# Another line for the time of a TensorE product in a kernel that orders its own instructions

## The chip, the cores and the metric

The kernel runs on one core of a Trainium2 chip. The number that counts is the device time of one execution in microseconds (us), as the median of several runs.

## What is computed

The kernel makes one inference step of a trunk of four layers, for 512 prompt frames and 32 sample frames side by side. Each layer normalises and modulates its input, mixes tokens, adds the result to the residual, normalises again and applies a gated feed forward (FFN). Layers 0 and 3 mix by differential attention, layer 1 by an mLSTM, layer 2 by latent attention.

```python
def trunk(x, c, past, p):
    ...
    for i in range(DEPTH):
        kind, j = i % N_MIXERS, i // N_MIXERS
        mod = (jax.nn.silu(c) @ p['w_ada'][i] + p['b_ada'][i])[:, None, :]
        sh1, sc1, gt1, sh2, sc2, gt2 = jnp.split(mod, 6, axis=-1)
        h = rmsnorm(x, p['g_norm1'][i]) * (1.0 + sc1) + sh1
        ...
        x = x + gt1 * out
        h = rmsnorm(x, p['g_norm2'][i]) * (1.0 + sc2) + sh2
        x = x + gt2 * swiglu(h, p['w_ffn_in'][i], p['w_ffn_out'][i])
    y = rmsnorm(x, p['g_final'])
```

## The kernel before

**Tiles.** Activations lie with features on the 128 partitions and the 544 frames along the row. A row is worked in two halves (`HALVES`): half 0 has 256 frames, half 1 has 288. Every operand of a large product is kept as a high and a low part (`hh` and `hl` for the input of a projection, `wh` and `low` for a weight), and `prod` issues three TensorE products for one K tile: high by high, low by high, high by low. A projection of one output tile and one half is 8 K tiles, so 24 products, added up in one PSUM bank (`mm`, `S` or `O` in the names).

**Norms.** `Norm.add` squares each new residual tile (`sq`) and sums it (`ss`). When the last output tile of a half is in the residual, `final_norm_task` is spawned with the highest priority. Its first step, `Norm.rstd`, makes two products with a matrix of constants (`T<-ss,ones_d` and `T<-sq,ones_d`), which add over the partitions; ScalarE makes `rs` of that, and `Norm.column` makes `ht`, `hh` and `hl`, one K tile at a time, on VectorE and ScalarE. In a mixer's output projection the last tiles go half by half, so the norm of half 0 is made while half 1 is still being projected, and the norm of half 1 while the FFN's first products on half 0 run. Those first products are a pair of PSUM tiles, 48 products on half 0.

**Who sets the order.** All of it is written by a scheduler in the kernel's own code. `Sched.run` holds the tasks, which are generators that issue TensorE's work, and an estimated time `t`. At each step it takes, among the tasks whose operands are estimated to be ready at `t`, the one of highest priority, and lets it issue its next products. `Tensor._held` estimates how long one product holds TensorE and moves `t` on by that. The instructions of VectorE (DVE), ScalarE (ACT) and GpSimd (POOL) get the first free time after their operands by `Engine.cost`, DMAs by their size. At the end of a phase everything noted is issued in the order of its estimated time. On the chip each engine then works through its own list in that order and waits on semaphores: an instruction that is not ready holds up those behind it on its engine, and the estimate plays no further part.

The norm's two products are asked for with `t_need`, which is a free bank and the time at which `ss` and `sq` are estimated to be written:

```python
    def final_norm_task(norm, i, finish):
        a, b = HALVES[i]
        yield t_need(norm.ss[:, a:b], norm.last[a][:, : b - a])
        yield from finish(norm, i)
```

**Other places named below.** In the mLSTM layer, `gates` is a long chain of small operations on VectorE and ScalarE; `turn_gates` and `sample_setup` bring its results through TensorE (`b_decb`, `hTl`, `b_rowsS`, `b_ash`). At the start, `warm_up` issues products without a use while the first loads come in, until the estimated time passes 16 us.

Of the kernel before, what the change touches and what calls it, by code (L numbers as in the profile page):

```python
# [13 lines left out]
PSUM = bass.MemoryType.PSUM  # L14

P = 128
# [35 lines left out]
def EARLY(h, z):  # L52
    """How many of the first conditioning's tiles are made after a projection."""
    return 0 if h == 0 else 2 if z == 2 and h < 4 else 1


class Sched:
    """An order of all engines' work, from an estimate of when each instruction can run.

    Tasks are generators that issue the tensor engine's work; each yields when its next step can start: None or a  # L60
    function that gives the time. The other engines' instructions take the first free time after their operands.
    Instructions are noted first and issued by their time, a phase at once.
    """
# [29 lines left out]
    def later(self, gen):  # L93
        """Work that only takes time that is left: yields its engine, what it reads and its cost, then notes it."""
        self.idle.append([gen, next(gen)])
# [17 lines left out]
    def flush(self):  # L113
        """Issues what is noted, in the order of its time."""
        self.log.sort(key=lambda a: a[:2])
        for _, _, issue in self.log:
            issue()
        self.log = []
        for eng, rows in self.busy.items():
            self.floor[eng] = max([self.floor.get(eng, 0.0)] + [b for _, b in rows])  # L120
# [7 lines left out]
    # what is known of a tile: (first and last partition, first and last column, time)  # L128
# [42 lines left out]
    def free(self, key, bufs):  # L171
        """When a new tile of a ring can be written."""
# [3 lines left out]
    def ready(self, *aps):  # L176
        """When the tensor engine can read."""
# [9 lines left out]
    def hole(self, eng, t, cost, take=True):  # L187
        """The first free time of an engine, from t on."""
# [60 lines left out]
class Engine:  # L249
    """An engine whose instructions are noted with their time."""  # L250
# [50 lines left out]
class Tensor:  # L301
    """The tensor engine, with an estimate of how long it is held."""
# [4 lines left out]
    def _held(self, out, lhs, rhs, passes, issue, turn=False):  # L307
# [8 lines left out]
        else:  # L316
            cost = max(passes * m / 2400.0, m / 1200.0, passes * n / 2400.0) + 0.0025
# [18 lines left out]
def tile_trunk(ctx: ExitStack, tc: tile.TileContext, I, O):  # L336
# [31 lines left out]
    class Banks:  # L368
        """PSUM banks for products and turned tiles, each use in the one that is free first.

        A bank for turned tiles is written and read before another one is asked for; one for products is shut.
        """
# [47 lines left out]
    def t_need(*aps):  # L420
        """A bank for turned tiles, and the operands."""
# [8 lines left out]
    def s_pool(es, shape, bufs):  # L430
        """Two PSUM banks of one phase: a pair in one tile, or one after the other."""
# [43 lines left out]
    # ---------------------------------------------------------------- loads  # L475
# [46 lines left out]
    # ---------------------------------------------------------------- weights  # L522
    def all_weights():
        """Every loaded weight, in the order of its use; some are split by GpSimd, where VectorE has much else to do."""
# [44 lines left out]
    class Feed:  # L569
        """Weights, loaded and split in place as soon as those before them are used up; some stay as they are."""  # L570
# [4 lines left out]
        def first(self, n):  # L575
            """The first ones' tiles; who takes them loads and splits them."""
# [55 lines left out]
    def units(us, started=False):  # L632
        """us: [(psum, parts)] side by side, one K tile of each at a time."""
# [21 lines left out]
    # ---------------------------------------------------------------- adaLN rows  # L655
# [5 lines left out]
    def ada_rows(ps, raw, first=0):  # L661
        """Four sums over K tiles in rows 32 g + (prompt, sample)."""
# [46 lines left out]
    # ---------------------------------------------------------------- residual and norms  # L709
    class Norm:  # L710
# [26 lines left out]
        def half(self, i, am, sh, silu=False):  # L737
            """The normed, modulated input of the next products: high and low parts of one half."""
# [33 lines left out]
    class Cycle:  # L772
        """PSUM banks in turn where no attention needs its own."""
# [18 lines left out]
    def out_block(load, drop, parts, gt, get, order, norm=None, finish=None, gate=None):  # L792
        """One block of K tiles of an output projection, added to the residual."""
# [26 lines left out]
    def paired():  # L820
        """K blocks of four tiles, two output tiles to a load: how to get one and how to drop it."""
# [15 lines left out]
    # ---------------------------------------------------------------- feed forward  # L837
# [80 lines left out]
    # ---------------------------------------------------------------- attention helpers  # L918
    def row_softmax(pool, ps, n, nk, scale, outs, masked):
        """ps: [P, n, >=nk] scores; outs[s] = exp(scale * (S - row max)); returns 1 / row sums."""  # L920
# [15 lines left out]
    def times_v(pool, pr, v, po):  # L936
        """po[dv, q] = sum over keys of v[key, dv] * pr[qt][q, key], 128 keys at a time."""
# [21 lines left out]
    def sample_times_v(p, vs, lock, pt, out):  # L959
        """p: [(h, q), 288] -> PSUM [(h, q), dv]; vs: [P, 3, 4, P] (last block: the new 32 keys)."""  # L960
# [18 lines left out]
    class Progress:  # L979
        """What has been issued, for the tasks that wait for it."""  # L980
# [21 lines left out]
    def rope_task(pool, pr, key, ps, i, hi, lo, r, perm, cos, sin, bufs=2):  # L1002
        """ps: one half of a projection; its rotation goes through the tensor engine in two exact parts."""
# [29 lines left out]
    # ---------------------------------------------------------------- differential attention  # L1033
    def layer_a(l, j, finish, early, first):
        lam_init = 0.8 - 0.6 * math.exp(-0.3 * l)
        with ExitStack() as es:
# [32 lines left out]
            def first_rows(k):  # L1069
                """The weights that make scale and shift of one K tile."""  # L1070
# [6 lines left out]
            def first_column(k, parts, am, norm):  # L1077
                """Scale and shift of one K tile, from the conditioning; then that tile of the input."""
# [1327 lines left out]
```

## Time and profile before

| | us |
|---|---|
| median of 3 runs (2749.83 to 2750.35) | 2750.12 |
| span of the profiled execution | 2748.0 |
| TensorE busy in it | 2705.6 |
| VectorE busy in it | 1820.7 |
| ScalarE busy in it | 1086.5 |

The span runs from the first to the last instruction of the core and is 2.1 us under the median of the runs, which also count what lies around it. TensorE's products overlap: a product of 256 columns shows about 0.28 us from start to end while its neighbour starts long before it ends. So its rate is read from the distance of two starts, and its waits from the idle time in front of an instruction, not from the busy share.

### The profile page before, as it was taken

What the parts mean: (1) busy time and instruction counts of PE and PEld (TensorE: products, weight loads), DVE (VectorE), ACT (ScalarE), POOL (GpSimd) and SP (SyncE); (2) the same over time, 40 slices, a digit from 0 to 9 for tenths busy, and PEclk for the clock granted to TensorE, in tenths of its full rate; (3) what the DMA queues carried; (4) which work ended last, traced back from release to release, by engine and by line L of the source; (5) the groups of instructions that cost most, each with busy time, mean ns of one, the idle gap of its engine ahead of it and who ended that gap; (6) DMA issues with size and microseconds to landing.
All of it is one profiled execution on the core that took longest, in us unless ns stands there. A gap on an engine that the chain in (4) does not pass through costs nothing.

```text
span 2748.0 us, 51869 instructions
## 1 busy us (share of the span) xinstructions
PE 2705.6 (98%) x21223; PEld 2590.8 (94%) x21223; DVE 1820.7 (66%) x3621; ACT 1086.5 (40%) x2382; POOL 238.0 (9%) x242
## 2 busy tenths in 40 slices
PE   9999999999999999999999999999999999999998
PEld 6888899999999999999998899999998899999998
DVE  6878777777665677777366767777558887433333
ACT  4555442122466442223255534222235554321222
POOL 1000300000200120000110020000031112000001
PEclk9999999999999999999999999999999999999999
DMA  8343244555222235455221124555333222222221
GB/s 281 129 139 123 87 153 164 187 172 180 87 83 78 76 110 174 170 183 176 80 97 33 47 78 142 170 181 177 126 108 97 77 80 75 77 88 90 88 86 68
DMA packets 101461, 330.94 MB, mean 120 GB/s; under 512 B 12840, under 2 KB 20140, under 8 KB 100840
## 3 DMA queue, kind: packets, MB, share of 16 engines
q1 hardware_dynamic: 95976, 309.48, 33.6%
q0 software_dynamic: 5248, 18.14, 1.8%
q8 instruction: 167, 2.74, 0.4%
q14 instruction: 70, 0.57, 0.1%
HBM read 314.69 MB, written 12.89 MB: 119 GB/s over the span
## 4 chain that ended last, share of the span: by engine, by line
PE 90%; DVE 6%; ACT 2%; issue 1%; DMA 0%; DVEq 0%; SPq 0%; ACTq 0%
PE mm L329 54%; PE S L329 21%; PE O L329 11%; PE T L329 2%; PE T L332 2%; DVE ht L296 1%; DVE hl L296 1%; DVE x L296 1%; ACT hh L296 1%; ACT wh L296 0%; DVE low L296 0%; DVE rq L296 0%; DVE mx L296 0%; DVE ql L296 0%; ACT rs L296 0%
## 5 line engine op out<-in xcount | busy, mean ns | idle before, releaser
L329 PE MATMUL mm<-hh,wh 128*128 128x288 f32 (+1 forms) x3078 | 909.8, 296 | 0.5 <-ACT hh L296 0.4
L329 PE MATMUL mm<-hh,low 128*128 128x288 f32 (+1 forms) x3078 | 887.9, 288 | 0.0
L329 PE MATMUL mm<-hl,wh 128*128 128x288 f32 (+1 forms) x3078 | 884.5, 287 | 2.2 <-DVE hl L296 2.2
L329 PEld LDWEIGHTS mm<-hh,wh 128*128 128x128 f32 x3078 | 580.7, 189 | 22.3 <-issue 15.1
L329 PEld LDWEIGHTS mm<-hl,wh 128*128 128x128 f32 x3078 | 581.8, 189 | 2.6 <-DVE hl L296 2.6
L329 PEld LDWEIGHTS mm<-hh,low 128*128 128x128 f32 x3078 | 581.1, 189 | 3.3 <-issue 2.4
L296 ACT CAST wh<-raw 128x1024 fp32r<-128x1024 f32 (+2 forms) x392 | 399.9, 1020 | 335.7 <-PE mm L329 159.4
L296 DVE TENSOR_TENSOR low<-raw,wh 128x1024 fp32r<-128x1024 f32 (+2 forms) x358 | 421.8, 1190 | 153.4 <-ACT wh L296 152.0
L329 PE MATMUL S<-hh,wh 128*128 128x288 f32 (+1 forms) x892 | 257.5, 289 | 0.5 <-ACT hh L296 0.5
L329 PE MATMUL S<-hl,wh 128*128 128x288 f32 (+1 forms) x892 | 256.6, 288 | 1.0 <-DVE rq L296 1.0
L329 PE MATMUL S<-hh,low 128*128 128x288 f32 (+1 forms) x892 | 257.3, 288 | 0.0
L329 PE MATMUL mm<-uh,wh 128*128 128x288 f32 (+1 forms) x836 | 241.3, 289 | 0.0
L329 PE MATMUL mm<-uh,low 128*128 128x288 f32 (+1 forms) x836 | 240.5, 288 | 0.0
L329 PE MATMUL mm<-ul,wh 128*128 128x288 f32 (+1 forms) x836 | 239.9, 287 | 0.0
L296 ACT CAST uh<-uf 128x256 fp32r<-128x256 f32 (+1 forms) x176 | 73.9, 420 | 406.1 <-DVE uf L296 405.9
L296 DVE SCALAR_TENSOR_TENSOR x<-mm,mod,x 128x256 f32<-128x256 f32 (+1 forms) x278 | 103.7, 399 | 163.3 <-PE mm L329 162.4
L296 POOL TENSOR_TENSOR ss<-ss,sq 128x256 f32<-128x256 f32 (+1 forms) x80 | 75.6, 945 | 1537.2 <-ACT sq L296 1536.9
L296 DVE CUSTOM_DVE_ANT_0 ada<-ada,sc,bada 128x1024 f32<-128x1024 f32 x152 | 194.7, 1281 | 2.6
L296 DVE CUSTOM_DVE_ANT_0 junk<-ada,sc,bada 128x1024 f32<-128x1024 f32 x152 | 194.5, 1280 | 1.0 <-DMA ada<-in_w_adaT 0.9
L329 PEld LDWEIGHTS S<-hh,wh 128*128 128x128 f32 x892 | 167.5, 188 | 2.8 <-issue 2.1
L329 PEld LDWEIGHTS S<-hl,wh 128*128 128x128 f32 x892 | 168.1, 189 | 1.8 <-DVE rq L296 1.3
L329 PEld LDWEIGHTS S<-hh,low 128*128 128x128 f32 x892 | 167.6, 188 | 0.0
(487 smaller groups left out, 5212.5 us busy)
## 6 DMA issues: line engine op xcount, KB each, us to landing
raw<-in_w_fin SPq DMA_DIRECT2D x176, 512.0 KB, 3.3
ada<-in_w_adaT SPq DMA_DIRECT2D x152, 512.0 KB, 4.5
raw<-in_w_fo SPq DMA_DIRECT2D x64, 512.0 KB, 3.3
raw<-in_w_qkv SPq DMA_DIRECT2D x45, 512.0 KB, 3.8
raw<-in_w_ada SPq DMA_DIRECT2D x24, 512.0 KB, 3.7
raw<-in_w_fl SPq DMA_DIRECT2D x32, 384.0 KB, 3.1
raw<-in_w_bh SPq DMA_DIRECT2D x24, 512.0 KB, 3.5
raw<-in_w_ao SPq DMA_DIRECT2D x16, 512.0 KB, 3.6
```

The source lines that it names most:

```text
L296: return s.work(self.kind, outs, ins, self.cost(name, args, kw, outs, ins), lambda: f(*args, **kw))
L329: lambda: self.pe.matmul(out, lhsT, rhs, start=start, stop=stop))
L332: self._held(out, in_, ident, 0, lambda: self.pe.transpose(out, in_, ident), True)
```

## The change

One line of `Tensor._held` is replaced. It is the estimate for every product of the split operands and for the wide products in full precision; the lines for turning a tile and for the narrow conditioning products stay. For 256 columns the estimate goes from 0.109 to 0.118 us, for 288 columns from 0.1225 to 0.132 us. All other differences of the two files are comments and docstrings.

```diff
         elif m <= 32 and passes == 4:
             cost = 0.02 + 0.053 * n / P
         else:
-            cost = max(passes * m / 2400.0, m / 1200.0, passes * n / 2400.0) + 0.0025
+            cost = max(passes * m / 2400.0, m / 1200.0, passes * n / 2265.0) + 0.005
         s = self.sched
         if s.t < COLD:
             cost *= 2
```

The instructions are the same, but for 8 of the `warm_up` products at the start, which are no longer issued (20754 products in place of 20762). What moves is the order, in nearly all of the mixers' stretches on every engine. Three places follow, with rows of each engine's list (source line, operation, output<-inputs with the tile's number, size of the output).

**From a mixer to its FFN, TensorE (first layer).** `mm_1044` is the last tile of the output projection, half 1; `mm_4770` and `mm_4771` (then `mm_4762` and `mm_4763`) are the FFN's first pair on half 0. Before:

```order
L329 MATMUL mm_4771<-hh,wh_1025 128x256
L329 MATMUL mm_4771<-hh,low_66 128x256
L329 MATMUL mm_4771<-hl,wh_1025 128x256
L329 MATMUL T_4772<-ss_1001,ones_d 128x288
L329 MATMUL T_4772<-sq_1046,ones_d 128x288
L329 MATMUL mm_4770<-hh,wh_1000 128x256
L329 MATMUL mm_4770<-hh,low_65 128x256
L329 MATMUL mm_4770<-hl,wh_1000 128x256
L329 MATMUL mm_4771<-hh,wh_1025 128x256
L329 MATMUL mm_4771<-hh,low_66 128x256
L329 MATMUL mm_4771<-hl,wh_1025 128x256
L329 MATMUL mm_4778<-hh,wh_1032 128x256
```

In the changed kernel:

```order
L329 MATMUL mm_4763<-hh,wh_1025 128x256
L329 MATMUL mm_4763<-hh,low_66 128x256
L329 MATMUL mm_4763<-hl,wh_1025 128x256
L329 MATMUL T_4764<-ss_1001,ones_d 128x288
L329 MATMUL T_4764<-sq_1046,ones_d 128x288
L329 MATMUL mm_4762<-hh,wh_1000 128x256
L329 MATMUL mm_4762<-hh,low_65 128x256
L329 MATMUL mm_4762<-hl,wh_1000 128x256
L329 MATMUL mm_4763<-hh,wh_1025 128x256
L329 MATMUL mm_4763<-hh,low_66 128x256
L329 MATMUL mm_4763<-hl,wh_1025 128x256
L329 MATMUL mm_4762<-hh,wh_1000 128x256
```

The norm's two products stood behind 42 of the pair's 48 products and stand now behind 30 of them: 12 products earlier, with 18 of the pair left behind them in place of 6. The same counts hold in all four layers.

**The same place, VectorE.** These are the last instructions ahead of and including the sum `ss` that the norm's product reads. Before:

```order
L296 TENSOR_TENSOR low_68<-raw_62,wh_1039 128x1024
L296 SCALAR_TENSOR_TENSOR ht_1042<-x,amod_1019,rs_1002 128x256
L296 SCALAR_TENSOR_TENSOR x<-mm_1041,mod_97,x 128x256
L296 SCALAR_TENSOR_TENSOR x<-mm_1044,mod_97,x 128x32
L296 SCALAR_TENSOR_TENSOR hl<-ht_1042,mod_97,hh 128x256
L296 SCALAR_TENSOR_TENSOR x<-mm_1044,mod_97,x 128x256
L296 TENSOR_TENSOR ss_1001<-ss_1001,sq_1043 128x288
```

In the changed kernel:

```order
L296 TENSOR_TENSOR low_68<-raw_62,wh_1039 128x1024
L296 SCALAR_TENSOR_TENSOR ht_1041<-x,amod_1019,rs_1002 128x256
L296 SCALAR_TENSOR_TENSOR x<-mm_1042,mod_97,x 128x256
L296 SCALAR_TENSOR_TENSOR x<-mm_1042,mod_97,x 128x32
L296 SCALAR_TENSOR_TENSOR hl<-ht_1041,mod_97,hh 128x256
L296 SCALAR_TENSOR_TENSOR x<-mm_1044,mod_97,x 128x256
L296 TENSOR_TENSOR ss_1001<-ss_1001,sq_1043 128x288
```

One small residual step changes its place. From the first `ht` of half 0 to this sum VectorE has 32 instructions before and 32 of the same kinds now, in each of the four layers.

**From an FFN to the next mixer, TensorE (into the mLSTM).** `mm_9072` to `mm_9074` are the mixer's first three tiles on half 0. Before:

```order
L329 MATMUL mm_9074<-hl,wh_5151 128x256
L329 MATMUL mm_9072<-hh,wh_5138 128x256
L329 MATMUL mm_9072<-hh,low_67 128x256
L329 MATMUL mm_9072<-hl,wh_5138 128x256
L329 MATMUL T_9076<-ss_5108,ones_d 128x288
L329 MATMUL T_9076<-sq_5160,ones_d 128x288
```

In the changed kernel, where the tiles are `mm_9068` to `mm_9070`:

```order
L329 MATMUL mm_9070<-hh,wh_5144 128x256
L329 MATMUL mm_9070<-hh,low_63 128x256
L329 MATMUL mm_9070<-hl,wh_5144 128x256
L329 MATMUL T_9071<-ss_5100,ones_d 128x288
L329 MATMUL T_9071<-sq_5153,ones_d 128x288
L329 MATMUL mm_9068<-hh,wh_5130 128x256
```

The pair stands 3 products earlier: 27 products lie between the FFN's last product and it, where there were 30. The same holds at all three such places.

## Rows read from the trace of the kernel before

**Rows 1.** The page: span, and busy time by engine (share of span).

```profile
span 2748.0 us, 51869 instructions
PE 2705.6 (98%) x21223; PEld 2590.8 (94%) x21223; DVE 1820.7 (66%) x3621; ACT 1086.5 (40%) x2382; POOL 238.0 (9%) x242
```

**Rows 2.** Busy time by stretch: start, mixer 0, FFN 0, mixer 3.

```profile
core 0: us, PE busy (x) PEld busy (x) DVE busy (x) ACT busy (x) POOL busy (x), PEclk, DMA share, GB/s
0.00:50.00 50.00, 48.00 (x339) 33.45 (x339) 26.87 (x96) 24.63 (x65) 9.26 (x17) 1.00 0.92 315
50.00:342.00 292.00, 285.25 (x2440) 253.50 (x2440) 241.03 (x589) 154.60 (x419) 35.60 (x39) 1.00 0.36 125
342.00:740.00 398.00, 397.15 (x3165) 396.87 (x3166) 285.99 (x461) 120.32 (x195) 18.02 (x17) 1.00 0.48 161
2048.00:2339.00 291.00, 280.84 (x2132) 254.53 (x2130) 246.22 (x555) 156.62 (x407) 59.53 (x57) 1.00 0.26 85
```

**Rows 3.** TensorE's waits by releaser: first four and last of 20.

```profile
engine line waited for: us in total, times, longest us
PE T L329 <- DVE ss L296: 12.9, 4, 3.3
PE T L329 <- DVE xl L296: 4.2, 7, 1.2
PE mm L329 <- DVE hl L296: 2.2, 2, 2.0
PE T L329 <- ACT sq L296: 1.8, 4, 0.7
...
PE T L329 <- ACT on L296: 0.3, 1, 0.3
```

**Rows 4.** TensorE in time order, mixer to FFN, layers 0 to 3.

```profile
start us, us, engine line op out<-in xcount [idle before <-releaser]
339.39 0.28 PE L329 MATMUL mm<-hl,wh 128*128 128x256 f32 x1
342.85 0.72 PE L329 MATMUL T<-ss,ones_d 128*128 128x288 f32 x2 [3.18 <-DVE ss L296]
343.68 0.49 PE L329 MATMUL mm<-hh,wh 128*128 128x256 f32 x1
...
996.50 1.03 PE L329 MATMUL T<-ss,ones_d 128*128 128x288 f32 x2 [3.32 <-DVE ss L296]
...
1650.51 0.72 PE L329 MATMUL T<-ss,ones_d 128*128 128x288 f32 x2 [3.24 <-DVE ss L296]
...
2339.49 1.30 PE L329 MATMUL T<-ss,ones_d 128*128 128x288 f32 x2 [3.19 <-DVE ss L296]
```

**Rows 5.** Busy time from the first `ht` to the `ss` sum, layers 0 to 3.

```profile
324.70:342.70 18.00, 14.96 (x118) 14.76 (x116) 17.88 (x32) 9.78 (x19) 10.72 (x9) 1.00 0.51 176
978.40:996.40 18.00, 14.78 (x117) 14.57 (x115) 17.84 (x33) 9.83 (x19) 11.06 (x9) 1.00 0.51 176
1632.40:1650.40 18.00, 14.86 (x118) 14.66 (x116) 17.84 (x32) 9.82 (x19) 11.04 (x9) 1.00 0.50 176
2321.30:2339.30 18.00, 15.01 (x118) 14.80 (x116) 17.84 (x32) 9.75 (x20) 10.70 (x8) 0.97 0.36 118
```

**Rows 6.** TensorE in time order inside FFN 0: starts of products, back to back.

```profile
384.83 0.30 PE L329 MATMUL mm<-hh,low 128*128 128x288 f32 x1
...
385.77 0.30 PE L329 MATMUL mm<-hl,wh 128*128 128x288 f32 x1
...
390.76 0.28 PE L329 MATMUL mm<-hh,low 128*128 128x256 f32 x1
...
391.94 0.28 PE L329 MATMUL mm<-hl,wh 128*128 128x256 f32 x1
```

**Rows 7.** TensorE at the first FFN's end, into the mLSTM.

```profile
740.94 0.75 PE L329 MATMUL T<-sq,ones_d 128*128 128x288 f32 x2 [0.33 <-ACT sq L296]
```

**Rows 8.** TensorE behind the mLSTM's gates.

```profile
776.71 0.25 PE L329 MATMUL T<-b_ash,b_selHr 4*128 4x32 f32 x1 [0.51 <-DVE b_tm L296]
```

**Rows 9.** Busy time and granted clock behind the waits of rows 4 and 8.

```profile
342.90:346.40 3.50, 3.50 (x26) 3.29 (x27) 2.37 (x4) 2.40 (x5) 1.11 (x3) 1.00 0.79 267
996.80:1000.20 3.40, 3.40 (x13) 2.91 (x12) 1.48 (x3) 1.62 (x3) 0.54 (x1) 0.50 0.84 296
1650.60:1654.00 3.40, 3.40 (x25) 3.19 (x26) 2.27 (x3) 2.31 (x4) 1.04 (x2) 1.00 0.72 258
2338.20:2345.00 6.80, 5.50 (x21) 4.96 (x22) 4.57 (x8) 4.56 (x9) 2.49 (x3) 0.50 0.00 0
778.30:785.10 6.80, 6.80 (x33) 6.80 (x33) 3.99 (x7) 3.25 (x6) 0.00 (x0) 0.50 0.12 26
```

## Prediction

> **What bounds the kernel now.** The page comes first: TensorE is busy for 98% of the span, VectorE for 66%, ScalarE for 40% [rows 1]. So VectorE and ScalarE matter only where TensorE waits for them, and the table by stretch says where that can be. In the first FFN TensorE is busy for 397.15 of 398.00 us; an order can win or lose nothing there. In the first mixer it is 285.25 of 292.00 and in the last 280.84 of 291.00 [rows 2]. Third, the list of who TensorE waited for: 20 kinds of wait that sum to 31.5 us. One kind alone is 12.9 us, four waits of up to 3.3 us for the sum `ss` on VectorE, and the next is 4.2 us in 7 waits [rows 3]. Fourth, these four waits in time order: they stand where a mixer hands over to its FFN, once in each layer [rows 4]. All that a new order can work on is 31.5 us of waits, the time at half clock that follows some of them, and new waits.
>
> **What the four waits are.** In rows 4 TensorE starts a product on half 0 of the FFN at 339.39 and then the norm's product at 342.85. The products behind it run at once afterwards; their input was there, but TensorE's list is worked in order. So the wait is not for want of work. It is there because the norm's product stands too early in the list. Its operand is late because VectorE has 32 instructions from the first `ht` to the sum, and they take exactly 18.00 us in each of the four layers, with VectorE busy for 17.84 to 17.88 of them [rows 5]. The moment at which `ss` is written is therefore set by VectorE's own list, not by TensorE.
>
> **The estimate against the trace.** In the FFN, ten products of 256 columns lie between the starts 390.76 and 391.94, so 0.118 us each; seven of 288 between 384.83 and 385.77, so 0.134 us [rows 6]. The old line says 0.109 and 0.1225, the new one 0.118 and 0.132: the new line is right about TensorE. But a scheduler that puts a waiting product in the list when its operand should be ready counts that delay in products. A slower TensorE means fewer products in the same delay, so everything that waits for another engine moves forward by some 8%, while the other engines' costs stay as they were. Where these are already too short, as at the four waits, the old error made up for part of it.
>
> [...]
>
> **The sum, part by part.**
>
> 1. Mixer to FFN, four times. The norm's products move forward by 12 products. VectorE has the same 32 instructions in both orders, so `ss` is not earlier, and TensorE gets there 12 x 0.118 = 1.42 us sooner and waits that much longer: about 4.7 us in place of 3.3. The 12 products are still to be done behind the wait, so nothing comes back, unless TensorE waited again at the end of half 0; it has no such wait now (the FFN stretch is busy but for 0.85 us, most of it this wait's end). 4 x 1.42 = **+5.7 us**. Bounds: 0 if VectorE's chain became shorter by as much, 6 if it became longer a little.
>
> 2. FFN to mixer, three times. The norm's products move forward by 3. The `sq` product waits 0.33 us there now [rows 7], so it is already at the edge: 3 x 3 x 0.118 = **+1.1 us**, between 0 and 1.1.
>
> 3. The mLSTM's gates. Of the 24 products of the tile ahead of `b_decb`, 18 stood in front of it and now 9 do, so TensorE comes up to 9 x 0.134 = 1.2 us earlier. The long gate chain is already waited for (0.51 us at 776.71) [rows 8]. Between 0 and 1.2; I take **+0.6 us**.
>
> 4. The clock. [...] The idle times were 3.32 and 3.19 us with the fall, 3.18 and 3.24 us without [rows 4], so the present length is just at the edge, and 1.42 us more should be over it at all four. Work at half clock takes twice its time: 5.50 / 2 = 2.75 us and 3.4 / 2 = 1.7 us lost, 2.2 on average. Two more such falls are **+4.4 us**. Bounds: 0 if none is added, and two of 6.8 us all busy, as in the third stretch of that kind [rows 9], so 6.8.
>
> 5. The other waits in the mixers, 31.5 - 12.9 - 1.8 = 16.8 us [rows 3]. Half of the distances there become shorter and others longer, since heads and rotations are interleaved anew. An 8% shorter lead of 2 to 5 us costs 0.2 to 0.4 us a place; a better interleaving can take single waits of 1 us away. I take **0**, between -8 (half of them gone) and +5.
>
> 6. The 8 missing products of the start: **0**. Loads hold that stretch, with 92% DMA share [rows 2]; if they did not, 8 products at 0.118 us would give back 0.9 us.
>
> Sum: 5.7 + 1.1 + 0.6 + 4.4 = 11.8 us. On the profiled execution's 2748.0 us that is 2759.8; what lies around the span (2.1 us to the median of the runs) does not change, so **2762 us** for the median.
>
> **The rivals.** A change under 0.2% (5.5 us) can hardly be told from none.
>
> - *The clock falls no oftener than now.* Terms 1 to 3 alone: 2757.5 us. The equal idle times with and without a fall speak for it: length alone does not decide. Against it, the waits grow by over 40%.
> - *The mixers' gain hides the boundaries' loss.* A TensorE that is timed rightly should interleave attention better. If half of the 16.8 us goes (-8), terms 1 to 3 are paid back, and with one more fall of the clock the time is 2752 us. For it: 7 of the waits are for the rotation's `xl`, up to 1.2 us [rows 3], and leads there change most. Against it: leads shrink on the whole.
> - *Faster.* The mechanism is the same, but TensorE's inner waits go almost wholly: 16.8 us less, 7.4 us more at the boundaries, no new fall of the clock, so 2741 us. It decides from 7.4 + 5.5 = 12.9 us on, over three quarters of the waits. [...]
> - *It does nothing.* If VectorE's list also ended earlier by 1.4 us at the boundaries, terms 1 and 4 are nil: 2750 to 2752 us. Against it stand the equal 32 instructions.
>
> **How the numbers follow.** All terms as summed, 2757 to 2768 us: 0.50. Boundaries without new falls of the clock, 2754 to 2759: 0.22, two thirds of it over 2755.6. Gain hides loss, or nothing happens, 2746 to 2754: 0.16. Faster, under 2744.6: 0.06. Worse inside the mixers, over 2768: 0.06. So slower by over 0.2%: 0.50 + 0.15 + 0.06 = 0.71; within: 0.07 + 0.16 = 0.23; faster: 0.06. The range from 2751 to 2769 leaves out about 0.18: the faster case, most of the upper one, and part of the third.
>
> **What would show it.** The wait of TensorE for `ss` should go from 12.9 us to some 18.5 in the list, still four times, now up to 4.7; the `sq` wait from 1.8 to nearly 3; VectorE's stretch to the sum should still be 18.0 us. The FFN's stretches should show half clock four times in place of twice. The FFNs themselves should have no new waits. If the four waits are not longer, step 1 is wrong and with it the forecast; if they are and the time is not, the mixers gave it back, and their idle time will show it.

## The result, and the profile after

The changed kernel takes 2776.76 us (median of 4 runs, 2776.53 to 2778.37) against 2749.97 us for the kernel before, run beside it (4 runs, 2749.45 to 2750.35): ratio 1.0097, 95% interval 1.0082 to 1.0111. It is 26.8 us slower. The direction was forecast and the size was not: 2762 was the forecast, 2769 the upper end of the range.

The page of the changed kernel, its first rows (span, busy time of each engine), which answer to [rows 1]:

```profile
span 2775.0 us, 51882 instructions
PE 2714.0 (98%) x21215; PEld 2595.9 (94%) x21215; DVE 1825.2 (66%) x3621; ACT 1088.3 (39%) x2382; POOL 235.4 (8%) x242
```

The span is 27.0 us longer; no engine has more instructions. TensorE's waits by releaser, from the first nine of 23 kinds, against [rows 3]:

```profile
engine line waited for: us in total, times, longest us
PE T L329 <- DVE ss L296: 19.1, 4, 4.9
PE T L329 <- DVE xl L296: 6.0, 10, 2.0
PE T L329 <- ACT sq L296: 4.5, 4, 1.3
PE S L329 <- ACT p L296: 3.6, 2, 1.8
PE O L329 <- DVE spt L296: 2.1, 2, 1.2
...
PE T L332 <- DVE pr L296: 1.6, 2, 1.2
PE T L332 <- DVE hn L296: 1.5, 1, 1.5
```

The kinds sum to 50.0 us, where they were 31.5. The wait for `ss` grew by 6.2 us, about as forecast. But `p`, 0.4 us in all before, is 3.6; `xl` went from 4.2 to 6.0 us and from 7 waits to 10; `pr` was not in the list. These stand inside the mixers.

TensorE in time order at the four mixer ends, against [rows 4]:

```profile
344.54 0.78 PE L329 MATMUL T<-ss,ones_d 128*128 128x288 f32 x2 [4.72 <-DVE ss L296]
...
1006.10 1.30 PE L329 MATMUL T<-ss,ones_d 128*128 128x288 f32 x2 [4.85 <-DVE ss L296]
...
1663.08 1.30 PE L329 MATMUL T<-ss,ones_d 128*128 128x288 f32 x2 [4.78 <-DVE ss L296]
...
2366.16 1.30 PE L329 MATMUL T<-ss,ones_d 128*128 128x288 f32 x2 [4.73 <-DVE ss L296]
```

Four waits of 4.7 to 4.9 us, as "about 4.7 in place of 3.3" said. The next view is a table by stretch, with columns as in [rows 2]: first VectorE's stretch from the first `ht` to the `ss` sum in layer 0, against [rows 5]; then the stretches behind these four waits and one in the mLSTM, against [rows 9]:

```profile
326.27:344.40 18.13, 13.55 (x106) 13.35 (x104) 18.00 (x32) 9.80 (x19) 9.78 (x8) 1.00 0.49 175
...
345.10:348.50 3.40, 3.40 (x15) 3.10 (x14) 2.02 (x3) 2.13 (x3) 1.34 (x3) 0.50 0.57 219
1003.80:1010.60 6.80, 4.50 (x16) 3.96 (x17) 4.80 (x10) 4.39 (x7) 2.29 (x4) 0.50 0.44 142
1662.60:1666.00 3.40, 2.92 (x9) 2.37 (x10) 1.82 (x2) 1.31 (x4) 1.32 (x2) 0.50 0.25 80
2365.80:2369.20 3.40, 3.04 (x9) 2.50 (x10) 1.69 (x2) 1.31 (x4) 0.69 (x1) 0.50 0.02 5
782.00:792.20 10.20, 10.09 (x42) 9.47 (x43) 5.22 (x16) 3.00 (x6) 1.18 (x1) 0.50 0.00 0
```

VectorE still needs its 18 us, and the clock is at 0.50 behind all four waits. In all, TensorE ran at 0.50 for 34.0 us in 7 stretches before its last products, where it was 17.0 us in 3. Two parts of the loss follow: 18.5 us more of waits, and 17.0 us more at half clock. Behind the first of the four waits, at 0.50, products of 256 columns start 0.214 us apart (eight steps between 346.51 and 348.22), where [rows 6] has 0.118 at 1.00. TensorE was busy in 15.1 us of the 17.0 (30.9 us after, 15.8 before); at that pace 45% of it is lost, an estimated 6.8 us. Together 25.3 of the 27.0 us by which the spans differ.

By stages, from one `ss` product on half 1 to the next, the loss lies in the mixers and above all in two of them: +1.7 us in the first (342.8 to 344.5, from the program's start), +5.3 in the mLSTM (256.5 to 261.8), +1.4 in the latent mixer (255.3 to 256.7), +11.6 in the last (291.9 to 303.5). Of each mixer's loss some 1.5 us is the longer wait for `ss` at its end, so that nothing is left in the first and the latent one. The four FFNs show +2.6, +1.6, +2.5 and +0.3. Waits of the last mixer, in time order:

```profile
2091.80 0.38 PE L329 MATMUL T<-xl,a_perm 128*128 128x256 f32 x1 [1.38 <-DVE xl L296]
2099.83 0.44 PE L329 MATMUL S<-kh,qh 64*128 64x384 f32 x2 [1.79 <-ACT p L296]
...
2158.64 0.40 PE L329 MATMUL T<-xl,a_perm 128*128 128x288 f32 x1 [2.05 <-DVE xl L296]
...
2309.97 0.50 PE L329 MATMUL S<-kh,qh 64*128 64x512 f32 x2 [1.83 <-ACT p L296]
```

So the first question is what makes waits inside the mixers, and why in these two.

### The profile page after: what moved, and what is told of

It is laid out like the page before. It is cut to its first block, busy times and chain, and to the rows that moved or that the text cites. A ratio compares the mean times of both kernels' runs of the same rounds, so it can differ in the third digit from the quotient of the medians.

```text
span 2775.0 us, 51882 instructions
## 1 busy us (share of the span) xinstructions
PE 2714.0 (98%) x21215; PEld 2595.9 (94%) x21215; DVE 1825.2 (66%) x3621; ACT 1088.3 (39%) x2382; POOL 235.4 (8%) x242
## 4 chain that ended last, share of the span: by engine, by line
PE 87%; DVE 9%; ACT 3%; issue 1%; DMA 0%; DVEq 0%; ACTq 0%
PE mm L329 51%; PE S L329 20%; PE O L329 11%; PE T L329 2%; DVE hl L296 2%; PE T L332 2%; DVE ht L296 1%; DVE mx L296 1%; DVE low L296 1%; DVE x L296 1%; ACT hh L296 0%; DVE pr L296 0%; ACT pr L296 0%; ACT wh L296 0%; ACT p L296 0%
## 5 line engine op out<-in xcount | busy, mean ns | idle before, releaser
L329 PEld LDWEIGHTS mm<-hh,wh 128*128 128x128 f32 x3078 | 582.2, 189 | 22.8 <-issue 15.8
L329 PE MATMUL S<-hl,wh 128*128 128x288 f32 (+1 forms) x892 | 256.7, 288 | 1.2 <-DVE rq L296 1.0
```

The costliest lines, as they stand in the source:

```text
L329: lambda: self.pe.matmul(out, lhsT, rhs, start=start, stop=stop))
```

## The experiments

The expectations of the first eight runs name two theories. **A** is the prediction's own: the other engines' estimates are too short, TensorE's too short one made up for it, and only the ratio of the two matters. **B** holds that the order before is to a good part a lucky draw, which any other line would lose.

### The line moved by half, by twice, and the other way

```diff
-            cost = max(passes * m / 2400.0, m / 1200.0, passes * n / 2265.0) + 0.005
+            cost = max(passes * m / 2400.0, m / 1200.0, passes * n / 2330.0) + 0.00375   # half
+            cost = max(passes * m / 2400.0, m / 1200.0, passes * n / 2145.0) + 0.0075    # double
+            cost = max(passes * m / 2400.0, m / 1200.0, passes * n / 2550.0)             # less
```

> The new line moved half way back to the old one: 0.1136 us for 256 columns. Theory A (the other engines' costs are estimated too short, so every step by which TensorE is estimated slower puts waiting products earlier and adds waits): between the two, about 2760 us; the waits for ss about 16 us in four (6 products earlier at the four mixer ends), and the other waits between 18 and 30 us. Theory B (only the fixed places at the layer ends count, and the rest of the loss is chance in how the attention heads happen to be interleaved): layer ends half of the loss, about 2756 us, with other waits anywhere from 15 to 35 us, without regard to the slope.

> The change made once more on top of itself: 0.127 us for 256 columns, which is over what the trace shows. Theory A: slower still, 2790 to 2805 us, since leads shrink by another 8%; the ss waits above 19 us and the other waits above 40 us. Theory B: the layer ends lose a little more (3 products more at the mixer ends, 6 at the FFN ends), the mixers are anywhere around where they are now: 2770 to 2785 us.

> TensorE estimated faster than before: 0.107 us (the floor of the line) for 256 columns and 0.113 for 288. Theory A: leads grow, other waits below the 18.6 us of before, time 2740 to 2750 us. Theory B: the mixer ends are as before (the norm's products stand at the same place), the FFN ends 6 products earlier (2 us), the mixers anywhere: 2747 to 2765 us.

Measured, beside a kernel before of 2749.86: half 2768.82 (ratio 1.0065, 1.0050 to 1.0080), double 2793.02 (1.0156, 1.0140 to 1.0171), less 2752.57 (1.0010, 1.0001 to 1.0020). The waits for `ss` follow the line: 6.8 us (less), 12.9 (before), 16.2 (half), 19.1 (after), 22.1 (double). With a still longer estimate it goes on getting worse, as A says. Not all of A's numbers came: half is 9 us over its 2760, and the waits beside `ss` are 37.2 us in double, where A had over 40. With a shorter one than before it did not get better: less gave 6.1 us of `ss` waits back and got others, of which these are the three largest beside `ss` (waits by releaser, kernel less):

```profile
PE mm L329 <- DVE hl L296: 7.9, 9, 2.0
PE T L329 <- DVE ss L296: 6.8, 4, 1.7
PE mm L329 <- ACT hh L296: 3.9, 6, 1.4
PE mm L329 <- DVE low L296: 3.4, 1, 3.4
```

A's number for less was wrong, and so was B's account of it, which left the mixer ends as they were: what is taken from one wait comes back as another, for the inputs that VectorE and ScalarE make beside the sum.

### The other engines' estimates stretched as well

The changed kernel, with the costs and delays of all other engines, of turned tiles and of narrow products 8% longer too:

```diff
-LAG = 0.13
-TO_PE = 0.13
+LAG = 0.1404
+TO_PE = 0.1404
...
     def work(self, eng, outs, ins, cost, issue):
+        cost = 1.08 * cost
```

> The changed kernel with the estimates of all other engines' work, of their delays and of TensorE's other products stretched by 1.08 as well, DMAs apart. Theory A: the ratio of TensorE to the others is that of before again, so the time is too, 2747 to 2755 us, with waits near 31.5 us and half clock for some 17 us. Theory B: the layer ends are as before, the mixers anywhere: 2745 to 2765 us. A third theory, that an estimate of TensorE close to its true pace is bad in itself, gives 2770 to 2780 us.

2750.18 us (1.0000, 0.9991 to 1.0010), the time of before, with `ss` waits of 12.2 us. The new line is not bad in itself, which puts the third theory out. What it breaks is a ratio; B allowed this time too.

### The new line in the FFNs alone, and in the mixers alone

```diff
-            cost = max(passes * m / 2400.0, m / 1200.0, passes * n / 2265.0) + 0.005
+            cost = (max(passes * m / 2400.0, m / 1200.0, passes * n / 2265.0) + 0.005 if self.sched.fitted
+                    else max(passes * m / 2400.0, m / 1200.0, passes * n / 2400.0) + 0.0025)
...
+            sched.fitted = False  # ahead of a mixer; True in the other kernel
             if l % 3 == 0:
...
+            sched.fitted = True   # ahead of an FFN; False in the other kernel
             yield from ffn(l, after_ffn, queue)
```

> The new line is used only while an FFN's products are issued, the old one in the mixers. TensorE's order inside the mixers is that of before; the norm's products at the mixer ends stand 3 products earlier (125 in place of 128 behind those of half 0) and those at the FFN ends 3 earlier. Theory A (leads in products are what counts): ss waits 12.9 + 4 x 0.35 = 14.3 us, sq waits up by 1 us, other waits as before (16.4 us); 2752 to 2757 us, the upper end if the clock falls oftener. Theory B (the loss is in the mixers' interleaving): 2751 to 2754 us.

> The new line is used only while a mixer is issued, the old one in the FFNs. The mixers have the changed kernel's order; the norm's products at the mixer ends stand 9 products earlier than before in place of 12. ss waits 12.9 + 4 x 9 x 0.118 = 17.1 us, other waits near the changed kernel's 26.4 us. Theory A and theory B: 2770 to 2776 us, most of the loss. If the FFNs' own order were the cause, under 2760 us.

FFNs alone: 2754.63 (1.0012, 1.0002 to 1.0021), with `ss` waits of 14.3 us and `sq` waits of 4.5. Mixers alone: 2778.87 (1.0101, 1.0086 to 1.0116), all of the loss, some 3 us over the upper end of what was expected. It is made while the mixers are put in order.

### What the clock costs at the mixer ends

Products without a use, on data that is there, ahead of the norm's products at the four mixer ends: 30 in the changed kernel, and 20 in the kernel before. They are issued, but not counted in the estimate.

```diff
         def rstd(self, a, b, fill=0):
             ps = t_bank()
+            for _ in range(fill):
+                PE.aside(ps[:, :256], hh[:, 0, 0:P], hh[:, 0, 0:256])
...
-            done = self.rstd(a, b)
+            done = self.rstd(a, b, FILL if i and silu else 0)
```

> The changed kernel with 30 useless products of 256 columns (30 x 0.118 = 3.5 us) ahead of the norm's products at the four mixer ends, where TensorE waits up to 4.9 us; they are no part of the estimate, so all else stays in order. If the falls of the clock there cost what term 4 says, about 2.2 us each with the granted clock at 0.50 afterwards, they vanish and 6 to 10 us come back: 2767 to 2771 us. If the clock there costs nothing (TensorE is not what ends that stretch), 2775 to 2778 us. If the products get in the way, more than 2778.

> The kernel before with 20 products without a use ahead of the norm's products at the four mixer ends (20 x 0.118 = 2.4 us, less than the 3.2 us wait). If the half clock behind these waits is what they cost beyond their length, the fall behind layers 1 and 3 (3.4 and 6.8 us, some 4.4 us of loss) goes and the time is 2745 to 2747, with the ss waits down to some 0.8 us each. If the fall comes from something else, it stays at 2750. If the 20 products push the norm back, 2752 or more.

The changed kernel so filled takes 2768.73 (1.0062, 1.0045 to 1.0079), 8.0 us less than without, or 9.6 us by the ratios, each to the kernel before beside it. The kernel before so filled takes 2744.81 (0.9980, 0.9971 to 0.9989), 5.4 us less than the 2750.21 beside it. The mean granted clock is 0.995 to 0.997 in the four runs of the changed kernel so filled, where it was 0.990 to 0.993 without, and 0.996 to 0.998 in the eleven of the kernel before so filled, where it is 0.994 to 0.997 in those beside it. In the kernel before the norm's product is not pushed back: it still waits for `ss` at all four, 3.0 us in all; in the changed kernel it still waits at two, 2.3 us, and may stand a little late at the others. So filling these waits is worth 8 to 10 us after the change and some 5 before it; that all of it is the half clock behind them was not shown. The difference is too small against these intervals to be set beside the prediction's 4.4. The rows of half clock say more: TensorE was busy for 13.9 us in those behind the four waits, against 8.9 before [rows 9], so by the pace measured above an estimated 2.2 us more are lost.

### The norm's product later

The kernel before, with the norm's products at the mixer ends asked for 1.6 us later, which puts them 15 products later:

```diff
-        yield t_need(norm.ss[:, a:b], norm.last[a][:, : b - a])
+        at = t_need(norm.ss[:, a:b], norm.last[a][:, : b - a])
+        late = getattr(finish, "late", 0.0) if i else 0.0
+        yield lambda: at() + late
```

> The kernel before, with the norm's products at the four mixer ends asked for 1.6 us later in the estimate: they stand 15 products later, all else as before. Theory A: each of the four waits falls from 3.3 us by 15 x 0.118 = 1.77 to 1.6, ss waits near 6 us, and no fall of the clock there: 7.1 us and up to 4.5 us, so 2738 to 2743 us. If the products behind it are then missing at the end of half 0 (TensorE waits for half 1 in their place), 2747 to 2750 us.

2759.05 us (1.0026, 1.0016 to 1.0035): slower, against both expectations. Its waits by releaser:

```profile
PE mm L329 <- ACT hh L296: 7.7, 5, 1.9
...
PE O L329 <- ACT hh L296: 2.9, 4, 0.8
PE O L329 <- DVE hl L296: 2.7, 4, 0.7
```

The wait for `ss` is gone, and 13.3 us of waits for `hh` and `hl` are there, on either side of the norm's product. The waits ahead of it, 1.8 to 1.9 us at each of the four ends, show that the product is not merely too early in the list: the `hh` of half 0, made from VectorE's `ht`, is late as well, and TensorE now runs into that. The 5.6 us behind it do not show this, for the edit moved more than the product. ScalarE in time order at the first mixer's end:

```profile
343.27 1.28 ACT L296 ACT_TABLE_LOAD   x1
344.57 0.38 ACT L296 ACTIVATE silu<-mm 128x256 f32<-128x256 f32 x1
345.87 1.28 ACT L296 ACT_TABLE_LOAD   x1
```

The FFN's first `silu` now stands ahead of the norm's `rs` (before, `rs` came first, at 344.09, and `silu` at 347.29), and ScalarE loads its function tables four times at each of the four ends in place of once, 12 loads of 1.28 us more in all (its list has 22, that of before 10). Half 1's `hh` stands behind them. So late is no clean test of the product's place.

### How far a small step goes, and whose estimate it is

Twice the line of before with its constant moved by 0.0005, and the changed kernel with VectorE's costs alone 8% longer:

```diff
-            cost = max(passes * m / 2400.0, m / 1200.0, passes * n / 2400.0) + 0.0025
+            cost = max(passes * m / 2400.0, m / 1200.0, passes * n / 2400.0) + 0.0020   # jig20
+            cost = max(passes * m / 2400.0, m / 1200.0, passes * n / 2400.0) + 0.0030   # jig30
...
     def work(self, eng, outs, ins, cost, issue):                                         # vector, on the changed kernel
+        if eng == "DVE":
+            cost = 1.08 * cost
```

> The kernel before with 0.0020 in place of 0.0025 in its old line, an estimate 0.4% shorter. Theory A (TensorE's estimate against the others' sets the waits, smoothly): within 1.5 us of before, waits of 30 to 33 us in all. Theory B (the order before is one good draw among many): any small move of the line loses some of it, waits of 36 to 44 us and 2752 to 2762 us.

> The kernel before with 0.0030 in place of 0.0025, an estimate 0.4% longer, a twentieth of the way to the change. Theory A: within 1.5 us of before plus 1 to 2 us (a twentieth of 27 us), so 2750 to 2753, waits of 31 to 34 us. Theory B: waits of 36 to 44 us and 2752 to 2762 us, no nearer to before than the half step was.

> The changed kernel with the estimates of VectorE's instructions alone 8% longer, all delays and the other engines' costs as they were. If VectorE's costs are the ones that are too short, most of the loss comes back as with all engines stretched: 2750 to 2757, the four ss waits back to some 3 us. If the fixed delays between engines are, little comes back: 2768 to 2777, ss waits of 4 us and more.

The small steps give 2752.83 and 2752.00 (both 1.0005, 0.9996 to 1.0014), with waits of 32.5 and 31.1 us. B is out for such steps by the waits: a nearby order is as good. With VectorE's costs longer the changed kernel takes 2755.96 (1.0018, 1.0009 to 1.0027): 20.8 of the 26.8 us come back, the `ss` waits fall to 13.9 us, the waits in all to 34.8. It is mostly VectorE's estimate that is too short; whose the other 6 us are was not tried.

### Why VectorE's estimate is too short

The scheduler's cost of an instruction with two operands of 256 columns and a scalar is 0.068 + 0.062 + 256 / 960 = 0.397 us. VectorE in time order in the first stretch of the changed kernel:

```profile
329.20 2.20 DVE L296 SCALAR_TENSOR_TENSOR hl<-ht,mod,hh 128x256 fp32r<-128x256 f32 x1
331.32 1.03 DVE L296 SCALAR_TENSOR_TENSOR ht<-x,amod,rs 128x256 f32<-128x256 f32 x1
...
332.93 0.48 DVE L296 SCALAR_TENSOR_TENSOR hl<-ht,mod,hh 128x256 fp32r<-128x256 f32 x1
333.33 0.48 DVE L296 SCALAR_TENSOR_TENSOR ht<-x,amod,rs 128x256 f32<-128x256 f32 x1
...
335.58 2.46 DVE L296 SCALAR_TENSOR_TENSOR ht<-x,amod,rs 128x256 f32<-128x256 f32 x1
337.97 1.03 DVE L296 SCALAR_TENSOR_TENSOR hl<-ht,mod,hh 128x256 fp32r<-128x256 f32 x1
```

and GpSimd beside it (idle time ahead in brackets):

```profile
328.72 2.40 POOL L296 TENSOR_TENSOR low<-raw,wh 128x1024 fp32r<-128x1024 f32 x1 [6.95 <-ACT wh L296]
331.08 0.98 POOL L296 TENSOR_TENSOR ss<-ss,sq 128x288 f32<-128x288 f32 x1
...
335.37 2.40 POOL L296 TENSOR_TENSOR low<-raw,wh 128x1024 fp32r<-128x1024 f32 x1 [0.89 <-ACT wh L296]
337.72 1.95 POOL L296 TENSOR_TENSOR ss<-ss,sq 128x288 f32<-128x288 f32 x2
```

From 332.93 to 333.33 an `hl` takes 0.40 us, just its estimate. The same `hl` at 329.20 takes 2.20 and an `ht` at 335.58 takes 2.46, and both end just behind a GpSimd instruction of 2.40 us, 0.28 and 0.27 us after it; behind them stand instructions of 1.03 us beside GpSimd's sums. The 32 instructions of the stretch are estimated at 11.8 us (23 of 0.397, 7 of 0.163, one split of 1.135, one sum of 0.368) and take 18.1. The prediction read this stretch as VectorE's own work. A third of it is time over the estimate, in which VectorE seems to be held up.

The same is seen in the last mixer. Three of its four waits shown above, at 2099.83, 2158.64 and 2309.97, stand behind one small VectorE step of the softmax, `mx` (two columns), which takes 0.17 us elsewhere (the median of the 102 in this trace). Two of the three, each with GpSimd's split beside it:

```profile
2096.38 2.35 DVE L296 TENSOR_SCALAR mx<-mx 128x2 f32<-128x2 f32 x1
2096.33 2.37 POOL L296 TENSOR_TENSOR low<-raw,wh 128x1024 fp32r<-128x1024 f32 x1 [7.05 <-ACT wh L296]
...
2306.26 2.39 DVE L296 TENSOR_SCALAR mx<-mx 128x2 f32<-128x2 f32 x1
2306.24 2.38 POOL L296 TENSOR_TENSOR low<-raw,wh 128x1024 fp32r<-128x1024 f32 x1 [10.72 <-ACT wh L296]
```

In the last mixer of the kernel before, nine other instructions of VectorE take over 2 us beside GpSimd's splits, but no `mx` takes more than 0.74.

The test takes GpSimd's work away from the mixer ends and gives it to VectorE, in the changed kernel (allvec_a) and in the one before (allvec_b). Its second line moves the sums of all norms, those at the FFN ends too:

```diff
 ON_POOL -= {(0, 2)}
+ON_POOL -= {(10 * l + 2, i) for i in (1, 2) for l in range(DEPTH)}
...
-                eng = eng or (G if j < KT - 2 else V)
+                eng = eng or V
```

> The changed kernel with GpSimd idle at the mixer ends: the norms' sums and the splits of the FFN's second and third weight, which GpSimd did, are given to VectorE, in the estimate and on the chip. VectorE's stretch to the half 1 sum is 18.0 us in the traces, while the scheduler's costs for its 32 instructions add up to 11.8 us; instructions of 0.40 us take up to 2.5 us there while GpSimd works. Theory G (GpSimd holds VectorE up, and that is what the estimate misses): although VectorE has some 8 instructions more to do, estimated at 4.4 us, its stretch falls to 16 to 17 us, the four ss waits from 4.8 to some 2 us each (8 us in place of 19.1), and the time to 2756 to 2765. Rival (VectorE's instructions are slow there by themselves, for instance behind the DMA traffic): the stretch grows to 20 us and more, the ss waits to 6 us each, and the time stays over 2776.

> The kernel before with the same work moved from GpSimd to VectorE. The norm's product then stands behind as many products as in the changed kernel with the same edit (121 since the product of half 0, by the two orders). Theory G: VectorE's stretch 16 to 17 us, ss waits of some 2 us each, 8 us in place of 12.9, time 2741 to 2749; the change then moves nothing at the mixer ends, and what is left between this kernel and the one with the change is the waits inside the mixers, 5 to 15 us. Rival: stretch 20 us or more, ss waits of 5 us and more, 2755 or more.

2759.27 us with the new line (1.0028, 1.0017 to 1.0039) and 2741.25 with the old one (0.9968, 0.9957 to 0.9980). Busy time of the first stretch, `ht` to `ss`, in allvec_b, with columns as before:

```profile
324.86:339.05 14.19, 13.54 (x106) 13.34 (x104) 14.02 (x33) 9.27 (x16) 0.32 (x1) 1.00 0.66 221
```

The sum now stands behind 3 splits and 5 other sums on VectorE and behind fewer steps of `ht` and `hl`: 33 instructions, estimated at 13.5 us (17 of 0.397, 7 of 0.163, 3 of 1.135, 6 of 0.368). They take 14.2. Estimate and trace differ by 0.7 us where it was 6.3; GpSimd is busy for 0.32 us in place of 9.78. The waits for `ss` are gone with both lines, all four. That is more than theory G expected. The rival, slow by themselves, is out for this stretch. The largest waits of allvec_b:

```profile
PE mm L330 <- ACT hh L297: 6.2, 9, 0.8
PE T L330 <- DVE xl L297: 4.1, 7, 1.2
PE mm L330 <- DVE hl L297: 3.6, 6, 2.0
```

Between the two there are still 18 us, where 5 to 15 were expected. The waits beside `ss` and `sq` are 33.7 us with the new line and 23.1 with the old, and the last mixer takes 301.6 and 288.9 us. GpSimd still splits weights there: ahead of the output projections the changed kernel's trace has 8 splits of 1024 columns on GpSimd in the last mixer (2065 to 2300 us) and 4 in the mLSTM (746 to 943), but 2 in the first mixer (50 to 280) and 1 in the latent one (1410 to 1600). The losses were 11.6, 5.3, 1.7 and 1.4 us. The last pair moves these to VectorE too:

```diff
-ON_POOL |= {(0, 3), (10, 9), (10, 15), (10, 21)} | {(30, 3 * h + 2) for h in range(1, 8)}
+ON_POOL = {(0, 3)}
...
-                eng = eng or (G if j < KT - 2 else V)
+                eng = eng or V
```

> The changed kernel with all splits of 1024 columns but one at the start, and the norms' sums, moved from GpSimd to VectorE, in the estimate and on the chip: those of the last mixer and of the mLSTM too, where the changed kernel lost most (11.6 and 5.3 us, against 1.7 and 1.4 in the two mixers with few splits on GpSimd). If GpSimd is what makes VectorE's estimate too short inside the mixers as well, the last mixer, 301.6 us with the mixer ends alone cleared, falls to 290 to 294, the other waits from 33.7 to 20 to 25 us, and the time to 2742 to 2750. If the waits inside come from something else (VectorE's own load, the fixed delays), the last mixer stays at 298 to 304 us and the time at 2755 to 2763.

> The same with the old line. If GpSimd makes the estimate too short inside the mixers: 2738 to 2743, within 6 us of the same kernel with the new line. If something else does: 2738 to 2743 too, or some us more for the longer work of VectorE, but 12 to 20 us under the same kernel with the new line, as with the mixer ends alone cleared (18 us).

New line: 2748.88 us (0.9994, 0.9985 to 1.0003). Old line: 2751.56 (0.9997, 0.9988 to 1.0006). With GpSimd's splits and sums out of the way the change costs nothing: by the ratios the new line gains some 28 us from the edit (1.0097 to 0.9994), and the old one stays where it was. The last mixer takes 294.0 us with the new line and 292.7 with the old; the waits are 30.3 and 30.1 us in all. The new line's time is as expected, its waits beside `ss` and `sq`, 29.6 us, are not (20 to 25); the old line came out some 9 us above the expectation. So of the 18 us between the pair with the mixer ends alone cleared, about half went because the new line gained (1.0028 to 0.9994) and about half because the old one lost (0.9968 to 0.9997). Most of the old line's waits are of one kind (waits by releaser, nogp_b):

```profile
PE mm L329 <- ACT hh L296: 16.5, 13, 6.3
```

One of them is 6.3 us long, at 2061.1, on the way into the last mixer. VectorE's greater load does not make it, for VectorE is idle there too:

```profile
2058.64 0.40 ACT L296 CAST hh<-hs 128x256 fp32r<-128x256 f32 x1 [5.12 <-POOL hs L296]
2059.39 0.21 DVE L296 TENSOR_SCALAR a_nlam<-a_ls 128x1 f32<-128x1 f32 x1 [4.75 <-ACT a_ls L296]
```

Both wait for GpSimd's `hs`, VectorE by way of ScalarE, and in GpSimd's list the loads of the last mixer's `ks` and `vs` stand right ahead of that. What makes the other waits was not tried. So GpSimd's help is worth having in some places, and allvec_b, with the sums and the FFN's splits moved and the old line, is the fastest of all: some 9 us under the kernel before, by its ratio.

## Why the prediction was wrong

**The mixer ends (term 1)** were right: forecast +5.7 us from 12 products, measured +6.2 (12.9 to 19.1), four times, 4.7 to 4.9 us each, behind a stretch of VectorE that stayed at 18 us. The explanation was incomplete. "Set by VectorE's own list" holds for the order of the list, but some 6 of its 18 us are GpSimd's doing (18.1 against an estimate of 11.8; in allvec_b, 14.2 against 13.5).

**FFN to mixer (term 2)** was too small: +1.1 forecast. TensorE in time order at the place of [rows 7]:

```profile
746.21 0.75 PE L329 MATMUL T<-sq,ones_d 128*128 128x288 f32 x2 [1.27 <-ACT sq L296]
```

0.33 became 1.27 us, and the same at the two other places, so some 2.8 us; the list of waits for `sq` goes from 1.8 to 4.5.

**The mLSTM's gates (term 3)**, +0.6, were about right: there is a new wait of 0.8 us for `b_dec_bc`, and the one for `b_tm` is still 0.5. The mixer lost 5.3 us, for other reasons: 1.5 us at its `ss` wait and 0.9 at the `sq` wait, its waits for `hn` and `Cl` longer by 0.5 and 0.4 us, and the half clock ahead of its first heads by 3.4 us.

**The clock (term 4)**, +4.4, was right in kind where it was put, too large there, and missed elsewhere. At the mixer ends the fall now comes four times in place of twice, for 17.0 us in place of 10.2, and TensorE's busy time in it gives an estimated 2.2 us of loss: "twice its time" was a little too much, as the products at 0.50 start 0.214 us apart against 0.118, which is 1.8 times. But 17.0 us of half clock also stand elsewhere, where there were 6.8: 4.6 us more. Of these, 10.2 us stand behind the mLSTM's gates, where there were 6.8, and 3.4 behind a wait for `p` in the last mixer; the prediction had nothing for either; the other 3.4, at 51.5 us, stand behind a wait of 2.0 us for `hl` that the kernel before has too, without a fall. The length of a wait did not decide: a fall stands behind the 1.8 us for `p` at 2309.97, and none stands behind 3.2 us in layers 0 and 2 of the kernel before. The bound of 6.8 us was for the ends alone; the whole comes to 6.8 too.

**The waits inside the mixers (term 5)** are the step that failed: "I take 0, between -8 and +5", measured +9.6 us (16.8 to 26.4 by its own count) before the clock. The argument named leads that shrink by 8%, priced a place at 0.2 to 0.4 us, and set that against a hoped-for better interleaving. The runs show places of another size: the two waits for `p`, 1.8 us each, and one for `xl`, 2.0, stand behind a step of 0.17 us that a split on GpSimd held for over 2.3. The old error in TensorE's estimate covered such hold-ups at least in part, and with the splits and sums moved to VectorE the new line costs nothing. The trace of before showed the reason: instructions of 0.48 us that take 2.2 us beside GpSimd (an `hl` at 327.62, beside a split of 2.39 us at 327.15). That the shorter leads brought these waits about follows from the runs with the line moved and with VectorE's estimate stretched; how far it is chance which instruction a split falls on was not tried.

**The missing warm-up products (term 6)** were rightly left out.

Of the rivals, "the clock falls no oftener" is out by the windows, "the mixers' gain hides the loss" and "faster" by the sign of term 5, and "it does nothing" by the longer `ss` waits. The case "worse inside the mixers, over 2768", given 0.06, is what happened.

What stays open: why less, which shortens the known waits, gets as much back in waits for `hh` and `hl` is read from its list and not tried by itself; what late would give without its table loads was not tried; and the scatter of a few us between orders of the same ratio (stretch has 21.6 us of waits beside `ss` and all `sq`, before 16.4, at the same time) is not explained by any of this.

## What to carry to other kernels

Where a program's order is made from estimates of several engines, the estimates must be right against each other; one that is made right alone can undo an error that was making up for another. Before correcting one, compare the estimate and the trace of the others over a whole stretch (11.8 against 18.1 us here), with the neighbours at work, not for one instruction alone. And where a wait looks like a product in the wrong place, ask first what holds up the engine that it waits for: moving the product, with the table loads that came with it, cost 7 us here (ratio 1.0026), and unburdening the engine gained 9 (0.9968).

## What the runs showed of the hardware

GpSimd holds VectorE up, which had not been expected of 32 small instructions with 8 neighbours: an `hl` of 0.40 us pace took 2.20 us beside a GpSimd split of 2.40 us, and with GpSimd out of the way 33 instructions took 14.2 us where 32 with less to do took 18. It shows on the forms with two tensors in SBUF, where all tiles of this kernel but TensorE's results (PSUM) lie (`ht`, `hl`), and on a TENSOR_SCALAR with one: `mx`, 0.17 us, took 2.33 to 2.39 us beside a split three times in the last mixer. A residual step that reads PSUM took 0.24 us, the mean of the 94 of its form, beside GpSimd's two sums of 337.72 to 339.67 us:

```profile
338.92 0.24 DVE L296 SCALAR_TENSOR_TENSOR x<-mm,mod,x 128x32 f32<-128x32 f32 x1
339.08 0.87 DVE L296 SCALAR_TENSOR_TENSOR hl<-ht,mod,hh 128x256 fp32r<-128x256 f32 x1
```

In the stretch of the changed kernel shown above VectorE is the second to start: the `hl` that started 0.48 us behind a split ended 0.28 us after it, and the `ht` that started 0.21 us behind one ended 0.27 us after it. What happens when GpSimd is the second was not shown.

Products without a use, in a wait that is there anyway, gave 5.4 us (interval of the ratio 0.9971 to 0.9989) in the kernel before, at a mean granted clock of 0.996 to 0.998 in place of 0.994 to 0.997. In late, twelve more loads of ScalarE's function tables, 1.28 us each, came with another order of `silu` and `rs` alone.
